# A hybrid decoder layer: attention takes the later chunk of each pair first, and chunk 2 is the last through the output stage

## The chip, the cores and the metric

The kernel runs on one core of one Trainium2 chip. The time is that of one execution on the device in microseconds; the median of three runs of the kernel before is 2466.35 us (2465.81 to 2468.02). The profile is of one further execution, which took 2469.59 us.

## The reference

One layer on a sequence of 2048 tokens of width 1024, all in float32. Cut to what matters:

```python
proj = x @ W_in                 # q, k, v (8 heads x 64), conv gates B, C, h, pooling input p
# attention, causal: token t sees s < t
z = q k^T / 8
log_om = log_sigmoid(-z)        # where s < t, else 0
tail = reverse_cumsum(log_om) - log_om
a = exp(log_sigmoid(z) + tail)  # stick breaking: sigmoid(z) times the product of what follows
attn_out = a v
conv_out = B * conv3(C * h);  pool_out = (window means - p) @ pool_w * pool_scale
mix = rmsnorm_per_64(concat(attn_out, conv_out, pool_out)) * gain
x = layer_norm(2**0.25 * x + mix @ W_o)
x = layer_norm(2**0.25 * x + square(relu(x @ W_up)) @ W_down)
```

## The kernel before

**Tiling.** The 2048 tokens are four chunks of 512. Each float32 operand of a dense product is split into a high part (a ScalarE copy to the type float32r) and a low part (a subtraction on VectorE or GpSimd), and a product is three matmuls: high by high, high by low, low by high.

**Attention.** A head of chunk `c` walks over the key segments `c, c-1, ..., 0` (`head`). Each segment has four units (`unit`), one for each 128 queries: two score matmuls into a bank `z` (L433, two buffers), two sigmoids (L436, L438), a scan along the keys that makes the running product (L443 on the diagonal segment, L446 elsewhere, which carries on from the segment before and reads one column of `z` as a dummy operand), and a multiply on GpSimd (L448). Each segment also has four blocks (`block`): transposes (L465), the split (L468, L469) and two matmuls with the values into `o` (L470, L471). So a head of chunk 0, 1, 2, 3 has 4, 8, 12, 16 units. `run` lays units and blocks out alternately, blocks five units behind. A head's end is `finish` (L484, L485); each pair of heads is then normalised (`rms`) and written to the scratch `mscr`, but for the last pair of all, which stays on the chip.

**Scratch in memory.** The projections write q, k and v to scratch tensors (`qscr`, `kscr`, `vscr`), and attention loads them by head and segment.

**Order of the program.** For the pair of chunks (0, 1), then for (2, 3): `qkv` projects keys, queries and values for heads 0 to 3 and then for heads 4 to 7, each for the lower chunk first; then attention runs for heads 0 to 3 of each chunk and for heads 4 to 7 of each chunk. After both pairs come the conv and pooling mixers (`bchp`, pairs (0, 1) and (2, 3)), the output stages of the four chunks (`out_stage`: mix times W_o, residual, layer norm, rows to `x1scr`; for chunks 0 and 1 also the transposed operands of the up projection to `tscr`), the up projection (`Up`; it reads the rows of chunks 2 and 3 back while it works on the first half) and the down projection.

**What sets the order of work.** Each engine has one queue, worked in order. A planner builds these queues ahead of time: it walks a modelled timeline and at each step issues the ready instruction of the highest priority. Attention stands above the dense products (`tc.high_priority(PRIO)`), and what evacuates a bank, loads operands or normalises stands above attention (`early`); within a class the order of the program decides. So projections, mixers and output stages fill TensorE wherever attention isn't ready. All DMAs are issued from SP's queue.

**The last output stage.** `out_stage(c)` for the last chunk loads seven of its eight mix tiles ahead (`ready`), does two banks of products on these seven, then takes the last pair's normalised product from the chip (`last_mix`, L512 to L514, in the buffers of the mix tiles), closes attention's pools and starts the up projection's loads. The first four output weights take the buffers of chunk 2's input tiles (`load_wo`); they are asked for where the last group of projections reaches the last chunk.

Of the kernel before, what the change touches and what calls it, by code (L numbers as in the profile page):

```python
# [22 lines left out]
NC = S // CH  # L23
HEADS = 8
HD = 64
ND = D // P
# [10 lines left out]
EORDER = (4, 5, 6, 7, 0, 1, 2, 3)  # L37
WINDOWS = (2, 4, 8, 16)
PRIO = 1 << 20
B11, T2, B21, T3, T1, T4, B22 = LOADS = range(7)  # L40
EARLY, LATE = 4, 6


def build(nc, tc, ctx, A, out):
# [78 lines left out]
    with ExitStack() as up:  # L123
        pools = phase1(nc, tc, ctx, up, A, ident, scr, hscr, split, rsqrt, layer_norm, bcast)
# [3 lines left out]
def phase1(nc, tc, whole, ctx, A, ident, scr, hscr, split, rsqrt, layer_norm, bcast):  # L128
# [39 lines left out]
    def early():  # L168
        return tc.high_priority(2 * PRIO)

# [32 lines left out]
    def defer(fn, groups):  # L203
        later.append([groups, fn])

    def tick():
        for item in later:
            item[0] -= 1
        while later and later[0][0] <= 0:
            later.pop(0)[1]()  # L210

    def dense_ps():
        return ppd.tile([P, CH], F, name="dn", tag="dn", bufs=2)
# [13 lines left out]
    def proj_t(xs, g):  # L227
        for c, w, x in operands(xs, g):
            for e in range(2):
                es = slice(e * P, (e + 1) * P)  # L230
                ps = dense_ps()
                for d in range(ND):
                    wh, wl = (t[:, d % 2, es] for t in w[d // 2])
                    xh, xl = x[d]
                    nc.tensor.matmul(ps, wh, xh, start=(d == 0), stop=False)  # L235
                    nc.tensor.matmul(ps, wh, xl, start=False, stop=False)  # L236
                    nc.tensor.matmul(ps, wl, xh, start=False, stop=(d == ND - 1))  # L237
                yield c, e, ps
                tick()
# [34 lines left out]
    def qkv(cs):  # L274
        xs = [(c, []) for c in cs]
        for g in range(2):
            proj_qk(xs, 2 + g, kscr, None)
            proj_qk(xs, g, qscr, 0.125)
            proj_v(xs, g)
# [31 lines left out]
    def bchp(chunks):  # L311
        x = [(c, []) for c in chunks]
        ys = {}
        mixers = {6: gate_b, 7: gate_c, 8: conv, 9: pool}
        for k, g in enumerate(GROUPS):
            for c, i, ps in proj_t(x, g):
                if c == NC - 1 and i == 0 and k == 3:
                    load_wo(EORDER[:4])
                with early():
                    mixers[g](c, i, ps, ys)  # L320
# [63 lines left out]
    def attention(c, pairs):  # L384
        for i in pairs:
            mix = {}
            for hh in range(2):
                head(c, 2 * i + hh, mix)

    def run(end=False):  # L390

        while units:
            units.pop(0)()
            turn[0] += 1
            if turn[0] > 5:
                blocks.pop(0)()
        while end and blocks:
            blocks.pop(0)()
            turn[0] = 0
        while end and soon:  # L400
            soon.pop(0)[1]()
# [89 lines left out]
    def load_wo(part):  # L491
        with early():
            w = [[load(A["w_o"][e][:, dd * CH:(dd + 1) * CH], "x", [P, CH], 2 * ND) for e in part] for dd in range(2)]
        wo.extend(zip(*w))

    def halves(name, tags, bufs=1):
        t = []
        for i, tag in enumerate(tags):
            h = pd.tile([P, CH], F, name=f"{name}_{i}", tag=tag, bufs=bufs)
            nc.sync.dma_start(h, A[name][i * CH:(i + 1) * CH].partition_broadcast(P))  # L500
            t.append(h)
        return t

    mix = {}

    def load_mix(c, part):
        with early():
            mix.setdefault(c, []).extend(load(mscr[c][e], "w", [P, CH], ND) for e in part)

    def last_mix(y):  # L510
        h = pm.tile([P, CH], R, name="mh", tag="wh", bufs=ND)
        nc.scalar.copy(h, y)  # L512
        l = pm.tile([P, CH], R, name="ml", tag="wl", bufs=ND)
        nc.vector.tensor_tensor(l, y, h.bitcast(F), ALU.subtract)  # L514
        mix[NC - 1].append((h, l))

    def out_product(c, ps, t, dd, part):
        ts = slice(t * P, (t + 1) * P)
        for i in part:
            (wh, wl), (mh, ml) = wo[i][dd], mix[c][i]  # L520
            nc.tensor.matmul(ps, mh[:, ts], wh, start=(i == 0), stop=False)
            nc.tensor.matmul(ps, mh[:, ts], wl, start=False, stop=False)
            nc.tensor.matmul(ps, ml[:, ts], wh, start=False, stop=(i == ND - 1))
# [1 line left out]
    g1, b1 = [], []  # L525

    def out_stage(c):
        ready = {0: 4, NC - 1: ND - 1}.get(c, 0)
        if c:
            load_mix(c, EORDER[:ready or ND])  # L530
        head = [dense_ps() for dd in range(2)] if ready else []
        for i, ps in enumerate(head):
            out_product(c, ps, i // 2, i % 2, range(ready))
        heads = len(head) // 2
        if c == NC - 1:
            pend.pop(0)(lambda fn: fn(), last_mix)
            att.close()
            ff.append(Up(nc, tc, whole, ctx, A, ident, x1scr, tscr, hscr))
            with early():
                ff[0].begin(pd)  # L540
        for t in range(4):
            r = pd.tile([P, D], F, name="r", tag="big", bufs=3)
            row = c * CH + t * P
            ld = nc.sync.dma_start(r, A["x"][row:row + P, :])
            if c == NC - 1:
                if t < 3:
                    with tc.issue_after(ld.ins):
                        ff[0].load(0, t)
            for dd in range(2):
                gs = slice(dd * 512, (dd + 1) * 512)  # L550
                ps = head.pop(0) if head else dense_ps()
                out_product(c, ps, t, dd, range(ready if t < heads else 0, ND))
                with early():
                    nc.vector.scalar_tensor_tensor(r[:, gs], r[:, gs], ALPHA, ps, ALU.mult, ALU.add)
                tick()
            if not g1:
                while later:
                    tick()
                g1.extend(halves("ln1_g", ("sqb0", "sqb1")))
                b1.extend(halves("ln1_b", ("rmsby", "rmsby"), 2))  # L560
            with early():
                layer_norm(pd, r, g1, b1)
                nc.sync.dma_start(x1scr[c][t], r)
            if c < 2:
                defer(lambda r=r, t=t: turn_out.rows(c, t, [r[:, 0:CH], r[:, CH:D]]), 2)
# [7 lines left out]
    for cs in ((0, 1), (2, 3)):  # L573
        qkv(cs)
        with tc.high_priority(PRIO):
            for pairs in ((0, 1), (2, 3)):
                for c in cs:
                    attention(c, pairs)
            run(True)
    for chunks in ((0, 1), (2, 3)):  # L580
        bchp(chunks)
    load_mix(0, EORDER)
    load_wo(EORDER[4:])
    with tc.high_priority(PRIO):
        while len(pend) > 1:
            pend.pop(0)(lambda fn: fn())
    ff = []
    for c in range(NC):
        out_stage(c)
    ff = ff[0]  # L590
    xw.close()
# [370 lines left out]
```

## Time and profile before

| | us |
|---|---|
| median of three runs | 2466.35 |
| lowest, highest | 2465.81, 2468.02 |
| profiled execution | 2469.59 |
| its span | 2467.8 |
| TensorE busy | 2404.1 |
| VectorE busy | 1590.3 |
| GpSimd busy | 1138.4 |
| ScalarE busy | 990.2 |
| mean granted clock of TensorE, as a share | 0.992 |

The span runs from the first to the last instruction of the profiled execution. Busy time is the union of an engine's instructions; the matmuls are pipelined, so that one whose own duration is 0.39 us can start 0.23 us after the one before.

### The profile page before, as it was taken

How to read it: one execution, taken by the hardware profiler on the slowest of the kernel's cores; microseconds unless marked ns; L12 is line 12 of the kernel's file. 1: busy time of each engine (PE TensorE's matmuls, PEld its weight loads, DVE VectorE, ACT ScalarE, POOL GpSimd, SP SyncE). 2: the span in 40 equal slices, each digit the busy share in tenths (PEclk: the TensorE clock that was granted, in tenths of full speed). 3: DMA queues.
4: the chain of work that ended last, by engine and by line, in shares of the span. 5: the costliest groups of instructions: out<-in, count | busy, mean ns of one | idle time of the engine just before them, and what ended most of it. 6: DMA issues, size and time to landing. Idle time of an engine off the chain costs nothing.

```text
span 2467.8 us, 33076 instructions
## 1 busy us (share of the span) xinstructions
PE 2404.1 (97%) x11728; PEld 1998.2 (81%) x11728; DVE 1590.3 (64%) x2243; ACT 990.2 (40%) x1913; POOL 1138.4 (46%) x833
## 2 busy tenths in 40 slices
PE   8999999999999999999999999999999999999997
PEld 6988888778778787788887888888778888888886
DVE  3778777888888899975767556655334333333367
ACT  4667666655765756512333222222112111111123
POOL 2557554864874856534656545554111101101137
PEclk9999999999999999999999999999999999999999
DMA  8658555623523456567665383333543212212212
GB/s 243 194 150 242 155 146 143 194 79 93 155 80 99 149 156 216 186 247 271 218 210 191 113 330 133 111 104 115 166 163 102 77 60 86 86 46 78 82 60 111
DMA packets 164854, 360.36 MB, mean 146 GB/s; under 512 B 18641, under 2 KB 35025, under 8 KB 162897
## 3 DMA queue, kind: packets, MB, share of 16 engines
q1 hardware_dynamic: 164688, 358.25, 45.3%
q8 instruction: 93, 1.52, 0.3%
q14 instruction: 73, 0.59, 0.1%
HBM read 245.19 MB, written 112.98 MB: 145 GB/s over the span
## 4 chain that ended last, share of the span: by engine, by line
PE 79%; DVE 9%; DMA 4%; POOL 3%; issue 3%; ACT 2%; SPq 1%; DVEq 0%; ACTq 0%; POOLq 0%
PE dn L891 8%; PE dn L893 8%; PE dn L892 8%; PE b L789 7%; PE c L789 4%; PE a L789 4%; PE z L433 4%; PE dn L235 3%; PE tp L465 3%; PE dn L237 3%; PE dn L236 3%; PE b L792 3%; PE c L792 2%; PE a L792 2%; PE o L471 2%
## 5 line engine op out<-in xcount | busy, mean ns | idle before, releaser
L448 POOL TENSOR_TENSOR g<-g,sig 128x512 f32<-128x512 f32 (+2 forms) x320 | 379.9, 1192 | 340.6 <-DVE g L446 154.5
L891 PE MATMUL dn<-d,ht 128*128 128x512 f32 x1024 | 399.6, 390 | 5.7 <-DVE y L895 3.2
L892 PE MATMUL dn<-d,ht 128*128 128x512 f32 x1024 | 399.1, 390 | 0.0
L893 PE MATMUL dn<-d,ht 128*128 128x512 f32 x1024 | 397.9, 390 | 0.5 <-DVE ht L869 0.5
L729 POOL TENSOR_TENSOR w<-raw,w 128x512 fp32r<-128x512 f32 x186 | 259.4, 1401 | 232.6 <-ACT w L728 232.5
L897 DVE TENSOR_TENSOR y<-dn,y 128x512 f32<-128x512 f32 x224 | 153.9, 688 | 323.8 <-PE dn L893 323.6
L855 POOL TENSOR_TENSOR d<-draw,d 128x1024 fp32r<-128x1024 f32 x32 | 76.7, 2411 | 518.4 <-ACT d L854 509.4
L446 DVE TENSOR_TENSOR_SCAN g<-beta,g,z 128x513 f32<-128x513 f32 x192 | 243.9, 1275 | 48.3 <-ACT sig L438 46.3
L868 ACT CAST ht<-draw 128x512 fp32r<-128x512 f32 x128 | 74.2, 620 | 447.2 <-PE dn L893 370.0
L436 ACT ACTIVATE beta<-z 128x512 f32<-128x512 f32 (+2 forms) x320 | 172.7, 540 | 164.3 <-PE z L433 152.5
L891 PEld LDWEIGHTS dn<-d,ht 128*128 128x128 f32 x1024 | 192.6, 188 | 47.7 <-DVE y L895 4.7
L893 PEld LDWEIGHTS dn<-d,ht 128*128 128x128 f32 x1024 | 192.7, 188 | 41.0 <-DVE ht L869 0.9
L892 PEld LDWEIGHTS dn<-d,ht 128*128 128x128 f32 x1024 | 192.6, 188 | 39.8
L728 ACT CAST w<-raw 128x512 fp32r<-128x512 f32 x186 | 114.4, 621 | 262.8 <-PE b L792 146.7
L235 PE MATMUL dn<-xh,wh 128*128 128x512 f32 x512 | 206.5, 406 | 8.0 <-ACT xh L182 4.9
L433 PE MATMUL z<-k,q 128*128 128x512 f32 (+3 forms) x640 | 193.5, 382 | 17.3 <-DVE g L446 13.0
L236 PE MATMUL dn<-xl,wh 128*128 128x512 f32 x512 | 206.6, 404 | 0.2 <-POOL xl L184 0.2
L237 PE MATMUL dn<-xh,wl 128*128 128x512 f32 x512 | 206.6, 404 | 0.0
L469 DVE TENSOR_TENSOR tl<-tp,th 128x512 fp32r<-128x512 f32 (+1 forms) x320 | 184.2, 595 | 32.0 <-ACT th L468 31.0
L465 PE MATMUL tp<-ident,g 128*128 128x128 f32 x1088 | 191.8, 275 | 2.0 <-POOL g L448 1.0
L789 PE MATMUL b<-x,w 128*128 128x512 f32 x768 | 190.1, 390 | 3.7 <-DVE u L796 2.1
L468 ACT CAST th<-tp 128x512 fp32r<-128x512 f32 (+1 forms) x320 | 161.6, 536 | 66.3 <-PE tp L465 53.9
(194 smaller groups left out, 4967.0 us busy)
## 6 DMA issues: line engine op xcount, KB each, us to landing
hscr<-h SPq DMA_DIRECT2D x128, 256.0 KB, 2.7
draw<-hscr SPq DMA_DIRECT2D x64, 512.0 KB, 4.0
raw<-in_w_up SPq DMA_DIRECT2D x62, 512.0 KB, 4.2
x<-tscr SPq DMA_DIRECT2D x14, 2048.0 KB, 13.1
wraw<-in_w_in SPq DMA_DIRECT2D x80, 256.0 KB, 3.3
k<-kscr SPq DMA_DIRECT2D x80, 256.0 KB, 3.1
v<-vscr SPq DMA_DIRECT2D x80, 256.0 KB, 2.9
xraw<-in_xt SPq DMA_DIRECT2D x64, 256.0 KB, 3.1
```

Of the source, the lines that this page charges most:

```text
L235: nc.tensor.matmul(ps, wh, xh, start=(d == 0), stop=False)
L236: nc.tensor.matmul(ps, wh, xl, start=False, stop=False)
L237: nc.tensor.matmul(ps, wl, xh, start=False, stop=(d == ND - 1))
L433: nc.tensor.matmul(z[:, 0:w], q[:, b, j * P:(j + 1) * P], m["k"][:, 0:w], start=(b == 0), stop=(b == 1))
L446: nc.vector.tensor_tensor_scan(left, rev, idle, st["prev"][j][:, OFF - 1:OFF], ALU.mult, ALU.bypass)
L448: nc.gpsimd.tensor_tensor(gv, gv, sig[:, 0:w], ALU.mult)
L465: nc.tensor.transpose(out=tp[:, j * P:(j + 1) * P], in_=m["g"][j][:, cols], identity=ident)
L729: self.nc.gpsimd.tensor_tensor(w[:, 1], src, w.bitcast(F)[:, 0], ALU.subtract)
L789: nc.tensor.matmul(ps, wk[:, 0, d], x[:, i, :, d, :], start=(first and d == 0 and i == 0), stop=False, skip_group_check=True)
L891: nc.tensor.matmul(ps, hh[:, ts], dh[:, ds], start=(i == 0), stop=False)
L892: nc.tensor.matmul(ps, hh[:, ts], dl[:, ds], start=False, stop=False)
L893: nc.tensor.matmul(ps, hl[:, ts], dh[:, ds], start=False, stop=(i == 3))
```

## The change

A constant `LAST = 2` replaces `NC - 1` (3) as the chunk whose output stage comes last: in the place where the output weights are asked for, in `last_mix` and in `out_stage`. The output stages run in the order 0, 1, 3, 2. Attention walks over a pair of chunks in reverse: 3 before 2, and, since the same loop serves both pairs, 1 before 0.

```diff
+LAST = 2
...
-                if c == NC - 1 and i == 0 and k == 3:
+                if c == LAST and i == 0 and k == 3:
                     load_wo(EORDER[:4])
...
-        mix[NC - 1].append((h, l))
+        mix[LAST].append((h, l))
...
-        ready = {0: 4, NC - 1: ND - 1}.get(c, 0)
+        ready = {0: 4, LAST: ND - 1}.get(c, 0)
...
-        if c == NC - 1:
+        if c == LAST:
             pend.pop(0)(lambda fn: fn(), last_mix)
...
-            if c == NC - 1:
+            if c == LAST:
                 if t < 3:
                     with tc.issue_after(ld.ins):
                         ff[0].load(0, t)
...
             for pairs in ((0, 1), (2, 3)):
-                for c in cs:
+                for c in cs[::-1]:
                     attention(c, pairs)
...
-    for c in range(NC):
+    for c in (0, 1, 3, 2):
         out_stage(c)
```

## Rows read from the trace of the kernel before

**Rows 1.** The page's first part: busy us, share of the span, instructions.
```profile
PE 2404.1 (97%) x11728; PEld 1998.2 (81%) x11728; DVE 1590.3 (64%) x2243; ACT 990.2 (40%) x1913; POOL 1138.4 (46%) x833
```

**Rows 2.** Busy time of each engine by stretch (us from the span's start).
```profile
core 0: us, PE busy (x) PEld busy (x) DVE busy (x) ACT busy (x) POOL busy (x), PEclk, DMA share, GB/s
78.00:198.00 120.00, 120.00 (x745) 106.44 (x745) 96.34 (x133) 81.10 (x179) 66.10 (x57) 1.00 0.62 171
331.00:455.00 124.00, 124.00 (x750) 108.47 (x749) 90.65 (x120) 83.52 (x173) 73.86 (x61) 1.00 0.60 164
455.00:850.00 395.00, 373.55 (x1911) 300.44 (x1909) 332.56 (x456) 245.29 (x497) 265.48 (x206) 0.98 0.36 112
850.00:1030.00 180.00, 172.87 (x897) 140.69 (x897) 173.65 (x254) 111.62 (x223) 114.42 (x90) 0.99 0.58 187
1030.00:1127.00 97.00, 94.41 (x429) 77.47 (x428) 69.59 (x129) 17.32 (x30) 32.51 (x26) 1.00 0.59 212
1127.00:1736.00 609.00, 605.31 (x2695) 501.11 (x2694) 374.71 (x442) 190.07 (x327) 334.70 (x238) 1.00 0.52 180
1736.00:2406.00 670.00, 663.89 (x2916) 547.63 (x2915) 264.80 (x411) 113.58 (x177) 95.44 (x40) 1.00 0.28 91
```

**Rows 3.** Waits of TensorE from 455 to 1030: us in total, times, longest.
```profile
PE z L433 <- DVE g L446: 13.0, 15, 3.8
PE o L471 <- DVE tl L469: 2.7, 4, 1.2
```

**Rows 4.** The last step of a head (L485), by stretch: length, busy (count).
```profile
331.30:472.00 140.70, 2.72 (x4) 1.00 0.62 177
472.00:693.00 221.00, 2.72 (x4) 0.98 0.34 103
693.00:836.50 143.50, 2.72 (x4) 0.98 0.33 101
836.50:1050.00 213.50, 2.73 (x4) 0.99 0.57 185
```

**Rows 5.** SP's queue at the starts: issue time, its length, line, operation.
```profile
77.65 0.81 SPq L427 DMA_DIRECT2D v<-vscr  x2
...
92.59 0.93 SPq L258 DMA_DIRECT2D vscr<-vst  x2
...
95.55 0.32 SPq L427 DMA_DIRECT2D v<-vscr  x1
...
194.86 2.21 SPq L258 DMA_DIRECT2D vscr<-vst  x2
...
218.29 0.93 SPq L258 DMA_DIRECT2D vscr<-vst  x2
...
312.83 0.93 SPq L258 DMA_DIRECT2D vscr<-vst  x2
...
337.05 0.93 SPq L258 DMA_DIRECT2D vscr<-vst  x2
```

**Rows 6.** The chain of waits near 200 us, then TensorE's timeline there.
```profile
199.77 4.79 DMA v<-vscr
...
201.83 1.05 PE L290 MATMUL msp<-blk,sqa 128*128 128x2 f32 x8
204.69 0.60 PE L470 MATMUL o<-th,v 128*128 128x512 f32 x1 [1.81 <-DMA v<-vscr]
205.09 0.63 PE L471 MATMUL o<-tl,v 128*128 128x512 f32 x1
...
208.29 0.30 PE L251 MATMUL dn<-wl,xh 128*128 128x256 f32 x1
```

**Rows 7.** The end of attention: first and last start of four steps.
```profile
L485 DVE TENSOR_TENSOR mixr<-o,mixr x32: 655/688/696, 86.4 to 1048.8; 64x512 f32<-64x512 f32 x32
L302 DVE SCALAR_TENSOR_TENSOR oa<-mixr,gain,msp x16: 695/734/748, 114.6 to 1063.0; 128x512 f32<-128x512 f32 x16
L512 ACT CAST mh<-oa x1: 613/613/613, 1086.1 to 1086.1; 128x512 fp32r<-128x512 f32 x1
L521 PE MATMUL dn<-xh,mh x8: 389/389/389, 1090.7 to 1126.2; 128*128 128x512 f32 x8
```

**Rows 8.** DMA issues: count, size, median us from issue to landing.
```profile
xraw<-in_w_o SPq DMA_DIRECT2D x16, 256.0 KB, 3.0
```

**Rows 9.** SP's queue: the last write of rows and the first reads.
```profile
1135.01 0.33 SPq L563 DMA_DIRECT2D x1scr<-r  x1
...
1148.91 1.66 SPq L718 DMA_DIRECT2D r<-x1scr  x3
```

## The prediction

> **What bounds the kernel now.** I began with the page's first part: TensorE is busy for 2404.1 of 2467.8 us, and no other engine comes near [rows 1]. Then the table by stretch [rows 2], whose edges I set where the chain of waits and the timeline of each stage change hands: projections alone to 78 us; attention with projections beside it to 455; attention with the conv and pooling mixers beside it to 850; attention with the output stages of chunks 0 and 1 to 1030; the other output stages to 1127; then the up and the down projection. From 1127 to 1736 TensorE idles 3.7 us in 609. The change touches the program only ahead of 1127 us, so whatever it brings must come out of the stretches before.
>
> There the reader is to see two kinds of stretch. From 331 to 455 TensorE is busy for 124.00 of 124 us while VectorE stands at 73%: attention is not what limits, since each time it waits a projection fills TensorE. From 455 to 850 TensorE idles 21.4 us (395 less 373.55) at a clock of 0.98, and from 850 to 1030 it idles 7.1 us (180 less 172.87) with VectorE at 96% (173.65 of 180). Those 28.5 us are the largest sum that a better order of attention could reach. The waits of TensorE between 455 and 1030 say what they are: 13.0 us in 15 waits of the score matmul for the scan that still holds its bank [rows 3].
>
> Next is the order of the heads. The last step of each head falls four times into each of these stretches [rows 4]: chunk 2, heads 0 to 3, takes 140.7 us; chunk 3, heads 0 to 3, 221.0; chunk 2, heads 4 to 7, 143.5; chunk 3, heads 4 to 7, 213.5. By the code a head of chunk 2 has 12 units and one of chunk 3 has 16, so a unit takes 2.93, 3.45, 2.99 and 3.34 us. A pace that goes with the chunk would show in the sum whichever comes first, so by itself the exchange only moves these four blocks about.
>
> **The change part by part.** No instruction is added or taken away: the same 320 units, 768 output matmuls and loads. What changes is which may start when, and with it the order in which the planner lays down each engine's queue up to 1127 us. The loop that is turned around serves both pairs of chunks, so chunk 1 also goes ahead of chunk 0.
>
> *Start of attention.* The first head now needs the values of chunk 1, whose second write goes out at 92.59 us; their first load goes at 95.55, where chunk 0's went at 77.65 [rows 5]. Attention starts up to 17.9 us later. In the meantime TensorE has the value projection and the next group's keys, which it ran anyway: 120.00 of 120 us busy from 78 to 198 [rows 2]. The attention work that stood between these projections moves behind them, so they end sooner; and scores and scans may run ahead of the values. I take 10 us of delay, between 0 and 17.9, and 0 us of TensorE time; without that cover it would be the 10.
>
> *Second group of heads, and chunks 2 and 3.* Here the values wanted first are written at 218.29 in place of 194.86, and at 337.05 in place of 312.83 [rows 5]: 23.4 and 24.2 us later by the old timing. But while attention is late, TensorE does just those projections. With its time fully used, an attention that is 10 us behind means projections that are 10 us ahead, and both meet again at the same sum of work. So I do not add these two to the first delay: 0 us, with up to 47.6 us of further delay as the other end (a rival below).
>
> *A stall at the second group.* At 199.77 attention loads values that have just been written, and the load lands 4.79 us later. TensorE, its queue in order, stands before the matmul that reads them: idle from 202.88 (201.83 plus 1.05) to 204.69, and the next 512-column matmul starts 0.40 us after it, in place of about 0.23, until 208.3 [rows 6]. That is 1.8 us of waiting, and by the doubled spacing of some 3.6 us after it another 1.8. With projections ahead of attention this wait should shrink; with chunk 1 first it can also return, since its values are the last written. I take half: −1.8 us, within −3.6 (gone) and +7.2 (once more at each of two starts).
>
> *The contended stretches.* Ten microseconds more of attention lie in the stretches where TensorE idles 28.5 us in 575: 10 × 28.5/575 = +0.5 us, at most +0.9 for the whole 17.9, at least 0.
>
> *The end of attention.* The last head ends at 1048.8, its normalised product is ready at 1063.0, and nothing takes it before 1086.1, when a buffer of the stage before comes free; the first matmul on it is at 1090.7 [rows 7]. So the end may come 23.1 us later at no price: 10 us are hidden, the cost is 0, and each microsecond beyond 23.1 is paid in full, because all but two banks of the last stage lie behind that product. That the last head is now a shorter one (12 units) buys nothing for the same reason. The stage that now stands third (chunk 3) has its mix complete 48 units before the end, as chunk 2 had 64 units before: at 2.99 us a unit that is 143 us ahead, ample.
>
> *Loads of the output weights.* They are asked for three projection units earlier, but their tiles are those of chunk 2's input, free only after its last unit, and they stand at the same place in the order of loads: 0 us; 16 loads of 3.0 us [rows 8] would be visible for one landing, +3.0, at the worst.
>
> *Rows of chunk 2.* They are now written last, up to 1135.01 by the old timing, and are the first that the up stage reads, from 1148.91 [rows 9], 13.9 us later. The first read is of the first row tile, written long before the last. 0 us; if a read met its own write, one landing, a few microseconds, on a transpose that stands beside full TensorE work.
>
> The sum: −1.8 + 0.5 = −1.3 us. The profiled execution took 2469.59 us, 1.8 around its span and 3.2 above the median of 2466.35. So 2468.3 as a profiled run, and 2465 as a median.
>
> One rule of the skill would put the ceiling elsewhere. The Trainium skill (Perfetto Trace Analysis, Identifying the Most-Contended Engine) says that the busy share of matmuls misleads, since they are pipelined, and that the busy share of weight loads is the better measure. Weight loads are busy 300.44 of 395 us (76%) from 455 to 850 against 501.11 of 609 (82%) in the full stage after [rows 2]; by that rule some 30 us of the first stretch are open in place of 21.4, an estimate that neglects the different mix of tile sizes. The sum stays the same by both; the faster rival's third would be about 12 us in place of 9.5, so 2453 in place of 2456.
>
> **The rivals.**
>
> *Slower: the delays add up.* If attention waits anew at each of its three starts, 17.9 + 23.4 + 24.2 = 65.5 us come together, 42.4 above the 23.1 of room: 2507. With two of the three, 42 us, 19 are paid: 2484. For it: in each group chunk 1 (or 3) is projected behind chunk 0 (or 2). Against it: a late attention hastens the projections, as above. It decides once the last head ends later than about 1072 us. I give it 0.13.
>
> *Slower: a new order with new stalls.* The planner sets the order from modelled times, and TensorE stands in real time before whatever is at the head of its queue. The 13.0 us that scores wait for scans [rows 3] are such a misfit. A re-laid queue could have as much again where long heads of chunk 3 now meet the mixers: +13, so 2478. For it: chunk 3's first four heads ran slowest (3.45 us a unit) in that very stretch. Against it: half of them now run before 455, beside projections. 0.17.
>
> *Faster: the new order fits better.* Chunk 3's first heads now start at about 340 us, so some 115 us of their long units lie in the stretch where TensorE is full and VectorE at 73%, and chunk 2's shorter ones fall among the mixers. If a third of the 28.5 us of idle time goes, 9.5 us are gained: 2456. Against it: the same number of units must still pass the later stretches. 0.30.
>
> That the change does nothing in effect, because the planner starts chunk 2's or 0's heads first as before, I put at under 0.02; the time would be the median of before.
>
> **How the numbers follow.** My forecast (moved about, hidden) has 0.40, the faster rival 0.30, the slower ones 0.30 together. What a measurement can tell from no change is about 0.2%, 4.9 us. The forecast's own spread is 2460 to 2470; a little of it on the fast side passes the bound, and some of each rival falls short of theirs: faster 0.33, same 0.37, slower 0.30. The range takes in 2456 and 2478 with the unknown terms beside them (−3.6 and +7.2 at the stall, +3.0 at the weights): 2450 to 2482, leaving out the added delays of 2484 and up.
>
> **What would show it.** Values of chunk 1 loaded first, near 85 to 95 us, with TensorE full from 78 to 198: the first step. No wait of TensorE for loaded values near 200 us, or a longer one: the stall. Last head ending between 1050 and 1072 us and the last product still waiting for its buffer: the room at the end. Idle time of TensorE from 455 to 1030 within 4 us of 28.5: the forecast against the second and third rivals. The up and down stages must keep their 609 and 670 us; if they do not, I missed a dependence there. I am wrong outright if attention ends past 1072 us with TensorE idle before the last stage, or if the stretch before 1127 is over 5 us shorter or longer.

## The result, and the profile after

The changed kernel takes 2482.86 us (median; 2479.59 to 2489.49) beside 2466.42 (2465.81 to 2468.02) for the kernel before: a ratio of 1.0073, 95% interval 1.0054 to 1.0092. It is 16.4 us slower where I had forecast no change. The profiled execution took 2484.28 us. In the fences of this kernel line numbers above L40 are one higher than in those of the kernel before (L433 is L434).

The page of the changed kernel, first part (busy time, share of the span, instructions), answers to [rows 1]:

```profile
span 2482.5 us, 33058 instructions
PE 2408.2 (97%) x11728; PEld 1999.2 (81%) x11728; DVE 1579.8 (64%) x2243; ACT 986.6 (40%) x1913; POOL 1144.1 (46%) x833
```

The span is 14.7 us longer, with the same number of instructions on each engine. The table by stretch, of the same kernel, answers to four rows of [rows 2] (columns as there; the up and down stages shifted by the 15.0 us by which they start later):

```profile
78.00:198.00 120.00, 119.73 (x743) 105.90 (x742) 86.89 (x117) 75.21 (x167) 60.31 (x53) 1.00 0.64 177
331.00:455.00 124.00, 123.78 (x738) 107.21 (x737) 92.55 (x118) 83.36 (x167) 72.94 (x58) 1.00 0.54 147
1142.00:1751.00 609.00, 606.66 (x2708) 502.32 (x2707) 378.42 (x443) 190.33 (x328) 337.51 (x239) 1.00 0.52 180
1751.00:2421.00 670.00, 662.77 (x2906) 546.67 (x2905) 262.70 (x411) 113.08 (x177) 93.20 (x40) 0.99 0.28 91
```

The up and down stages are as before (606.66 busy for 605.31, 662.77 for 663.89). All of the difference lies ahead of them. To find where, I cut both traces at the same events rather than at the same times: the first value projection, the first key projection of chunk 2, its counterpart for heads 4 to 7, the last value projection, the middle of the mixers, the last projection, the last head, the last output product. The first fence is the kernel before, the second the changed one; the first pair of numbers is the stretch and its length, the next TensorE's busy time.

```profile
0.00:55.90 55.90, 47.95 (x192) 37.40 (x193) 20.77 (x38) 24.26 (x39) 14.39 (x20) 1.00 0.82 235
55.90:212.90 157.00, 155.19 (x1014) 140.81 (x1013) 122.87 (x168) 103.33 (x234) 88.60 (x78) 0.99 0.67 189
212.90:332.70 119.80, 119.76 (x738) 105.66 (x737) 94.46 (x131) 81.97 (x177) 72.08 (x60) 1.00 0.63 179
332.70:454.50 121.80, 121.80 (x734) 106.39 (x733) 89.97 (x118) 81.53 (x170) 71.66 (x60) 1.00 0.60 163
454.50:648.40 193.90, 180.79 (x915) 145.28 (x915) 162.01 (x218) 116.17 (x235) 126.75 (x99) 0.97 0.36 112
648.40:846.90 198.50, 192.31 (x997) 155.13 (x996) 168.57 (x236) 126.57 (x258) 136.18 (x106) 0.98 0.36 112
846.90:1048.80 201.90, 191.41 (x986) 155.24 (x985) 191.57 (x282) 121.89 (x243) 124.84 (x98) 0.99 0.57 186
1048.80:1126.70 77.90, 76.52 (x344) 63.15 (x343) 54.15 (x104) 10.09 (x17) 25.13 (x20) 1.00 0.61 221
```

```profile
0.00:59.80 59.80, 49.23 (x192) 38.19 (x193) 21.00 (x38) 23.69 (x39) 14.40 (x20) 0.97 0.77 216
59.80:209.70 149.90, 147.74 (x954) 132.41 (x954) 107.01 (x147) 92.90 (x206) 76.94 (x67) 1.00 0.65 180
209.70:339.10 129.40, 126.30 (x781) 110.13 (x780) 101.20 (x148) 87.94 (x199) 82.52 (x69) 1.00 0.64 180
339.10:467.20 128.10, 125.75 (x742) 108.83 (x741) 96.10 (x120) 84.13 (x169) 74.38 (x59) 0.99 0.57 156
467.20:656.90 189.70, 181.44 (x930) 146.31 (x930) 160.17 (x222) 118.23 (x243) 129.54 (x102) 0.98 0.39 117
656.90:862.60 205.70, 191.38 (x985) 155.20 (x984) 167.13 (x235) 125.25 (x255) 138.86 (x107) 0.98 0.35 107
862.60:1068.70 206.10, 196.67 (x1010) 160.18 (x1009) 190.11 (x295) 121.32 (x245) 126.62 (x100) 0.98 0.58 189
1068.70:1142.00 73.30, 71.79 (x322) 59.20 (x321) 49.70 (x93) 8.95 (x15) 21.99 (x18) 1.00 0.61 221
```

Length less busy time is TensorE's idle time. Before, stretch by stretch: 7.95, 1.81, 0.04, 0.00, 13.11, 6.19, 10.49, 1.38, in all 41.0 us. After: 10.57, 2.16, 3.10, 2.35, 8.26, 14.32, 9.43, 1.51, in all 51.7. So 10.7 of the 15.3 us by which the output products end later (1142.0 less 1126.7) are idle time. No one stretch holds them: the first gives 2.6, the two in which TensorE had no idle time give 5.4, the first half of the mixers takes back 4.9 and the second half gives 8.1. The other 4.6 us are matmuls at a wider spacing, and 3.4 of them are the granted clock: read in windows of 1 us, busy time times what the clock lacks of 1.00 makes 15.0 us up to the last output product, where it made 11.6 before. Of these 3.4 us, 1.7 lie in the first stretch (0.97 for 1.00). The last 1.2 us are not placed.

What TensorE waits for, in us in total, times and longest. First the kernel before from 56 to 455 us, where this is its only wait, then the changed kernel from 59 to 467:

```profile
PE o L470 <- DMA v<-vscr: 1.8, 1, 1.8
```

```profile
PE z L434 <- DVE g L447: 3.0, 3, 2.1
PE o L472 <- DVE tl L470: 1.8, 3, 1.1
PE z L434 <- ACT sig L439: 1.1, 1, 1.1
PE o L471 <- ACT th L469: 0.9, 2, 0.5
PE o L471 <- DMA v<-vscr: 0.5, 1, 0.5
```

The reader is to see that the one stall I had priced (values just written) nearly went, and that nine small waits on attention's own chain came: a score for a bank that a scan or a sigmoid holds, an output product for its operand's high or low part. Each stands where the next instruction of TensorE's queue isn't ready; whether other work was ready just then, the rows do not say. Over the whole run the waits of scores for scans grew from 13.0 to 16.0 us, and those of output products for low parts from 3.8 to 9.2.

The end of attention, by first and last start, answers to [rows 7]:

```profile
L486 DVE TENSOR_TENSOR mixr<-o,mixr x32: 655/688/696, 116.5 to 1068.7; 64x512 f32<-64x512 f32 x32
L513 ACT CAST mh<-oa x1: 616/616/616, 1101.4 to 1101.4; 128x512 fp32r<-128x512 f32 x1
L522 PE MATMUL dn<-xh,mh x8: 389/389/389, 1105.9 to 1141.6; 128*128 128x512 f32 x8
```

The last head ends 19.9 us later and its product is taken 32.7 us after that: still not what the last stage waits for.

### The profile page after: what moved, and what is told of

The parts are those of the page before. It is cut to its first block, busy times and chain, and to the rows that moved or that the text cites. A ratio compares the mean times of both kernels' runs of the same rounds, so it can differ in the third digit from the quotient of the medians.

```text
span 2482.5 us, 33058 instructions
## 1 busy us (share of the span) xinstructions
PE 2408.2 (97%) x11728; PEld 1999.2 (81%) x11728; DVE 1579.8 (64%) x2243; ACT 986.6 (40%) x1913; POOL 1144.1 (46%) x833
## 4 chain that ended last, share of the span: by engine, by line
PE 76%; DVE 10%; DMA 5%; POOL 3%; issue 3%; ACT 2%; SPq 0%; DVEq 0%; ACTq 0%; POOLq 0%
PE dn L892 8%; PE dn L894 8%; PE dn L893 8%; PE b L790 6%; PE c L790 4%; PE a L790 4%; PE z L434 3%; PE dn L236 3%; PE dn L237 3%; PE dn L238 3%; PE b L793 3%; PE tp L466 3%; PE c L793 2%; PE a L793 2%; PE o L472 2%
## 5 line engine op out<-in xcount | busy, mean ns | idle before, releaser
L449 POOL TENSOR_TENSOR g<-g,sig 128x512 f32<-128x512 f32 (+2 forms) x320 | 386.2, 1211 | 343.5 <-DVE g L447 143.7
L434 PE MATMUL z<-k,q 128*128 128x512 f32 (+3 forms) x640 | 193.4, 383 | 20.9 <-DVE g L447 16.0
L470 DVE TENSOR_TENSOR tl<-tp,th 128x512 fp32r<-128x512 f32 (+1 forms) x320 | 185.2, 595 | 25.7 <-ACT th L469 24.9
```

The source lines that it names most:

```text
L434: nc.tensor.matmul(z[:, 0:w], q[:, b, j * P:(j + 1) * P], m["k"][:, 0:w], start=(b == 0), stop=(b == 1))
L449: nc.gpsimd.tensor_tensor(gv, gv, sig[:, 0:w], ALU.mult)
```

## The experiments

Two theories stood against each other. **Lateness**: attention starts later, since the chunk it takes first is projected last, and the delay is paid somewhere. **New queue**: no delay is paid; the planner lays the engines' queues down anew, and the new ones meet the chip's real times worse than the old ones. In the expectations, A and D are forms of Lateness and B is New queue; C puts the whole cost on the turn of chunks 2 and 3, and E on the long heads of chunk 1 ahead of the short ones of chunk 0. Each TensorE queue written out has some 8,100 rows; "lines of difference" below are rows removed and rows added against the kernel before, counted together (a row that moves counts twice, so 16,200 would be all). "Idle" is TensorE's idle time up to the last output product, found as above.

**Which part of the change costs.** The exchange has two parts, chunk 3 ahead of 2 and chunk 1 ahead of 0. `only23` keeps the first alone, in the changed kernel:

```
-                for c in cs[::-1]:
+                for c in (cs if cs[0] == 0 else cs[::-1]):
```

> Chunk 3 ahead of chunk 2 and the output stages in the order 0, 1, 3, 2 as in the change, but chunk 0 ahead of chunk 1 as before. The change cost about 14.7 us between the two profiled executions; counted against each matmul's own steady spacing, TensorE lost 3.8 us more before 62 us, 4.6 more from 186 to 248 and 7 more from 807 to 931. Theory A (the two starts of chunk 1 are to blame for the first two): the first two go, the third stays: about +6 to +8 us over the kernel before, 2473. Theory B (the new order of the queues, whatever it is, meets other stalls): no such split; anything from -5 to +20. Theory C (the turn in the pair 2, 3 is all of it): +14 to +17, 2482.

Measured: 2469.24 us (2467.68 to 2469.74), ratio 1.0011 (1.0002 to 1.0020); idle 42.1. `only01` puts the second part alone into the kernel before:

```
-                for c in cs:
+                for c in (cs[::-1] if cs[0] == 0 else cs):
```

> Chunk 1 ahead of chunk 0, but chunk 2 ahead of chunk 3 and the output stages in order as before. Theory A: both early losses are there (one 3.4 us wait for a bank near 36 us, short waits from 195 to 245), and little else: +8 us, 2474. Theory B: anything from -5 to +20, and the two halves don't add up to the whole. Theory C: +-3, 2466.

Measured: 2480.45 (2477.88 to 2481.57), ratio 1.0053 (1.0036 to 1.0070); idle 49.8. So in the queues laid down here, what the change is named after costs 2.8 us, and the turn of chunks 0 and 1, which came with the shared loop, 14.0. Theories A and C miss both times. Theory B allows both, but its halves were not to add up to the whole, and here they do: 16.8 us for 16.4.

`proj_rev` is the changed kernel with the projections turned too, so that the chunk wanted first is also the one whose values are written first:

```
-        qkv(cs)
+        qkv(cs[::-1])
```

> The changed kernel, with the projections of each pair also taken in reverse (chunk 1 ahead of 0, 3 ahead of 2), so that the values that attention wants first are again those written first. Theory A (attention asks for what is projected last): the first values are loaded near 78 us again, the early losses of 8.4 us go, about 2474. Theory B: the losses move elsewhere, no sure sign. Theory C: stays at 2480 or above.

Measured: 2478.71 (2474.66 to 2480.36), ratio 1.0046 (1.0031 to 1.0061); idle 49.3. Most of the loss (12.3 of 16.4 us) stays when the values come early, at 81.35 us for 99.26 in the changed kernel; Theory A had looked for 2474. `swap_pairs`, the kernel before with head pairs 0 and 1, and 2 and 3, exchanged, was to be a new order of equal work:

```
-            for pairs in ((0, 1), (2, 3)):
+            for pairs in ((1, 0), (3, 2)):
-EORDER = (4, 5, 6, 7, 0, 1, 2, 3)
+EORDER = (4, 5, 6, 7, 1, 0, 3, 2)
```

> The kernel before with no chunk exchanged: only the two pairs of heads of a group trade places (heads 2, 3 ahead of 0, 1, and 6, 7 ahead of 4, 5), with the mix tiles summed in that order. Every head has the same work, the same chunk order and the same dependences on projections. Theories A and C: no reason for a difference, within 3 us of 2466. Theory B: a new plan alone moves the time by 5 to 15 us, either way.

Measured: 2465.66 (2460.14 to 2473.40), ratio 0.9994 (0.9981 to 1.0007); idle 40.5. It tests less than I meant: the queues of the four computing engines come out the same instruction for instruction, only with other heads' addresses. What it shows is that the same queue gives the same time.

**Is it lateness?** `proj01_rev` turns only the projections of chunks 0 and 1, in the kernel before, so that attention gets the wrong chunk first there:

```
-        qkv(cs)
+        qkv(cs[::-1] if cs[0] == 0 else cs)
```

> The kernel before with attention in its own order (chunk 0, then 1), but the projections of the pair 0, 1 reversed, so that chunk 0's values are written last and attention starts late for that reason alone. Theory D (an attention that starts late leaves VectorE idle early, and the lack is paid later, where VectorE is 96% busy beside the output stages): the start is some 15 us late, the last head ends near 1060, about +8 to +14 us, 2477. Theory E (it is the long heads of chunk 1 ahead of the short ones of chunk 0 that disturb the queues, not the lateness): within 3 us of 2466.

Measured: 2475.02 (2474.20 to 2480.43), ratio 1.0035 (1.0024 to 1.0046); idle 50.7. By the time alone this is Theory D's forecast (+8 to +14 us), and Theory E misses. `early_v` goes the other way: query and value projections alternate chunk by chunk, so values come early. The two functions become generators that yield after each chunk (those lines are left out here).

```
...
-            proj_qk(xs, g, qscr, 0.125)
-            proj_v(xs, g)
+            for step in zip(proj_qk(xs, g, qscr, 0.125), proj_v(xs, g)):
+                pass
...
```

> The kernel before with the query and value projections of a group taken by chunk: q of the lower chunk, v of the lower chunk, q of the upper, v of the upper (before: both q, then both v). Chunk 0's values are ready two query projections (10.9 us of matmuls) sooner, and so are chunk 2's. Theory D turned round: an attention that starts earlier ends earlier, and time is gained: last head near 1038, -4 to -9 us, 2460. Theory E: within 3 us of 2466.

Measured: 2484.85 (2482.95 to 2486.42), ratio 1.0070 (1.0049 to 1.0090); idle 51.7. The last step of a head and the matmuls on the last product, first and last start, first in `proj01_rev`, then in `early_v`:

```profile
L485 DVE TENSOR_TENSOR mixr<-o,mixr x32: 654/688/695, 108.8 to 1077.6; 64x512 f32<-64x512 f32 x32
L521 PE MATMUL dn<-xh,mh x8: 389/389/389, 1098.7 to 1133.9; 128*128 128x512 f32 x8
```

```profile
L489 DVE TENSOR_TENSOR mixr<-o,mixr x32: 653/688/696, 81.1 to 1045.0; 64x512 f32<-64x512 f32 x32
L525 PE MATMUL dn<-xh,mh x8: 389/389/389, 1106.9 to 1141.9; 128*128 128x512 f32 x8
```

`early_v` starts and ends its heads earlier than the kernel before (81.1 for 86.4, 1045.0 for 1048.8) and loses 18.4 us, where Theory D had a gain of 4 to 9 and Theory E no change; `proj01_rev` ends them 28.8 us later and loses 8.6. So a loss as large as the change's needs no lateness. That some of the 8.6 us in `proj01_rev` is lateness is not excluded.

`g0_rev` and `g1_rev` turn chunks 0 and 1 for heads 0 to 3 alone and for heads 4 to 7 alone:

```
+                for c in (cs[::-1] if cs[0] + pairs[0] == 0 else cs):            # g0_rev
+                for c in (cs[::-1] if cs[0] == 0 and pairs[0] == 2 else cs):     # g1_rev
```

> The kernel before with chunk 1 ahead of chunk 0 for heads 0 to 3 alone (the first start, at 60 to 95 us). Theory D: most of the cost of reversing the pair 0, 1 (13.9 us) is here, since this is where nothing else is left for attention to do: +8 to +13, 2477. If the second start (the values near 200 us) carries it: +2 to +4, 2470.

> The kernel before with chunk 1 ahead of chunk 0 for heads 4 to 7 alone (the second start, near 200 us). Theory D: attention has caught up with the projections there (a load of just written values stalls it already), so it is late by some of the 23 us between the two chunks' values: +2 to +6, 2470. If the second start carries it all: +10 to +14, 2478.

Measured: `g0_rev` 2483.59 (2478.34 to 2484.18), ratio 1.0060 (1.0038 to 1.0082), idle 53.4; `g1_rev` 2474.15 (2470.31 to 2477.65), ratio 1.0024 (1.0012 to 1.0036), idle 47.3. The halves lose 17.2 and 7.7 us by their medians, together 24.9, where both at once lose 14.0. Costs that belong to each half by itself would add up; these don't. (A delay that both halves share would not add up either, so this alone does not decide.) Neither half falls where Theory D put it, +8 to +13 and +2 to +6.

**The old order of chunks, laid down anew.** If the queues are the cause, edits that leave the order of chunks alone must cost as much. `START` is a counter value at which the low parts of operands change the rule by which they are dealt to VectorE or GpSimd: 46 in place of 40 changes the engine of at most six of them (VectorE's instructions are 2,245 for 2,243), 37 and 43 of at most three. `lag6` lets attention's blocks run one unit further behind.

```
-START = 40
+START = 46        # start46; start37, start43 and start34 likewise
-            if turn[0] > 5:
+            if turn[0] > 6:        # lag6
```

> The kernel before with no chunk exchanged: of the loads numbered 40 to 45 alone, the low part is made by the other of VectorE and GpSimd (a constant of 40 becomes 46). No dependence changes, no work is moved by more than six operations of about 1 us, and attention starts as before; but the planner's queue for TensorE then differs from the old one over more than half its length (6185 lines of difference of some 8100, from line 898 on, before the second start). Theory B (the queues of the kernel before fit the chip better than a queue planned anew, and every new plan pays 5 to 15 us in TensorE's waits): +5 to +15, 2476, with the waits of the second matmul on values (for ScalarE's and VectorE's split) grown. Theory A or D (order and lateness of attention): within 3 us of 2466.

> As the run before, with the constant at 37: loads 37 to 39 alone change engine. TensorE's queue differs in 6838 lines. Theory B: +5 to +15, 2476. Theories A and D: within 3 us of 2466.

> The kernel before with attention's blocks six units behind the scores in place of five: one unit more in flight, the same work and chunk order. TensorE's queue differs in 6610 lines. Theory B: +5 to +15 like any new plan. Theories A and D: attention starts at the same time and waits less for its split, so 0 to -5 us, 2464.

Measured: `start46` 2476.00 (2475.24 to 2476.73), ratio 1.0044 (1.0029 to 1.0059), 6,185 lines, idle 45.5. `start37` 2481.88 (2479.11 to 2484.61), 1.0064 (1.0045 to 1.0083), 6,838 lines, idle 51.6. `lag6` 2489.18 (2488.31 to 2490.85), 1.0098 (1.0083 to 1.0113), 6,610 lines, idle 56.4. (The 6,185 lines are 38% of the queue, removed and added rows being counted together; "more than half" in the expectation counted them once.) The three edits, none of which has to do with the exchange, cost 9.6, 15.5 and 22.8 us against 2466.42. Theories A and D had looked for none. Theory B has the direction, but 15.5 and 22.8 lie above its 5 to 15, and the waits that it named did not grow in `start46` (output products for low parts 4.1 us for 3.8, scores for scans 6.0 for 13.0). Attention's end in `lag6`:

```profile
L485 DVE TENSOR_TENSOR mixr<-o,mixr x32: 654/688/696, 87.3 to 1040.1; 64x512 f32<-64x512 f32 x32
L521 PE MATMUL dn<-xh,mh x8: 389/389/389, 1112.9 to 1147.7; 128*128 128x512 f32 x8
```

The slowest kernel of all has the earliest end of attention.

> The kernel before with the constant at 43: TensorE's queue differs from the old one in 786 lines alone and comes back to it. Theory B: a queue that stays nearly the same costs nearly the same, within 4 us of 2466. If changing the engine of a load is what costs in itself (the constants 37 and 46 did 15 and 10 us): +5 or more, 2473.

> The kernel before with the constant at 34: 7518 lines of difference. Theory B: +5 to +20, 2479. If the cost came with particular loads near number 40 to 45: no reason for more than 3 us.

Measured: `start43` 2470.54 (2466.12 to 2473.75), ratio 1.0014 (1.0005 to 1.0023), only 786 lines, idle 45.0; `start34` 2484.60 (2481.06 to 2485.62), 1.0072 (1.0057 to 1.0087), 7,518 lines, idle 49.4. A queue that stays nearly the same keeps nearly the same time (4.1 us above 2466.42, just over the 4 of Theory B), and the three changed engines of `start43` cost a quarter of what the three of `start37` do: it isn't the change of engine that costs.

**The new order of chunks, laid down anew.** The same constant in the changed kernel, and in `only23`:

> The changed kernel with the constant at 46: again a new plan (6866 lines of difference to the changed kernel's) for the same order of chunks. Theory B: the cost of the change is that of a plan, so it moves: anywhere from 2470 to 2490, with no reason to stay at 2482. Theories A and D: the cost is in the order of chunks and stays, 2480 to 2485.

> The changed kernel with the constant at 34, a third plan of the new order. Theory B (the order has no cost of its own): it falls among the re-planned kernels of the old order, 2474 to 2489. If the new order has a cost of its own of 10 us or more on top of the plan's: 2485 to 2500.

> The turn of chunks 3 and 2 alone (it cost 2.7 us), with the constant at 46 (which cost 9.6 us alone and changes the queues from about 165 us on). Theory B: the early queue goes, and the cost with it rises to that of a new plan: 2474 to 2486. If the turn of 3 and 2 is free whatever the plan, and costs add: 2479.

Measured: `after_start46` 2483.61 (2478.15 to 2484.54), ratio 1.0070 (1.0052 to 1.0088), idle 47.7 in an execution of 2478.15; `after_start34` 2472.18 (2470.75 to 2477.84), 1.0031 (1.0021 to 1.0041), idle 46.6; `only23_start46` 2473.59 (2469.57 to 2476.42), 1.0032 (1.0019 to 1.0045), idle 42.9. With the same exchange of chunks, `after_start34` is 10.7 us faster than the changed kernel, and the intervals of their ratios lie apart. The constant that costs the old order 18.2 us takes 10.7 from the new one. `after_start46` decides nothing: it lies where both theories allowed it. The other two lie a little below Theory B's ranges (2472.18 for 2474 to 2489, 2473.59 for 2474 to 2486), and far from the costs that would stay (2480 to 2485) or add (2479). Paired by the constant, the new order is 16.4 us (40) and 7.6 us (46) behind the old one and 12.4 us (34) ahead of it, 3.9 us behind on average, far inside that spread: a cost of the order itself is not shown, and one of a few us is not excluded. The row of `after_start34` for all that lies ahead of the last output product, then that of the changed kernel:

```profile
0.00:1133.30 1133.30, 1086.71 (x5905) 908.20 (x5906) 901.88 (x1289) 661.15 (x1365) 668.86 (x538) 0.99 0.53 161
```

```profile
0.00:1142.00 1142.00, 1090.30 (x5905) 910.45 (x5906) 892.41 (x1291) 662.41 (x1365) 665.24 (x536) 0.99 0.53 160
```

**All together.** Over the 18 kernels (both given ones and these 16) the medians go with TensorE's idle time, correlation 0.90; with the end of the last head it is −0.05. That the time goes with how the queues happen to fit is shown by the edits that change little but the queues; the correlation by itself says less, since idle time is a part of the time. Most of the rest of the spread is the clock: read in windows of 1 us as above, it takes 6.1 to 19.3 us in the 18 profiled executions, and the end of the last output product less idle time and less this lies between 1072 and 1081 us in all of them, where the ends themselves run from 1126 to 1148. How much of the clock's part belongs to the queue is open; the kernel before, too, had 0.996 in an execution of 2461.65 us and 0.991 in one of 2469.38. Which entries decide, and why the kernel before has so little idle time between 213 and 455 us, stays open. None of these queues beat the kernel before: `swap_pairs`, with its queue, ties, and the others lie 2.8 to 22.8 us behind, 12.4 on average.

## Why the prediction was wrong, point by point

*Start of attention: right in its cost, low in its size.* The first values are loaded at 99.26 us, by SP's queue of the changed kernel (issue time, length; it answers to [rows 5]):

```profile
93.06 0.93 SPq L259 DMA_DIRECT2D vscr<-vst  x2
99.26 0.81 SPq L428 DMA_DIRECT2D v<-vscr  x2
```

That is 21.6 us after the old 77.65, more than the 17.9 I held for the most; I had looked for it near 85 to 95. Yet from 78 to 198 TensorE is busy for 119.73 of 120 us: the projections cover it, as I wrote.

*Second group, chunks 2 and 3: right.* The further 47.6 us of delay did not come. Attention's end moved by 19.9 us, no more than the start.

*The stall near 200 us: right about the stall, wrong about its neighbourhood.* The load's wait shrank from 1.8 to 0.5 us, and the doubled spacing behind it went (granted clock 1.00 from 199 to 213), but two other waits came near 200 us:

```profile
200.20 0.33 PE L472 MATMUL o<-tl,v 128*128 128x128 f32 x1 [0.54 <-DVE tl L470]
204.32 0.73 PE L434 MATMUL z<-k,q 128*128 128x512 f32 x2 [1.12 <-ACT sig L439]
```

*The contended stretches: inside my margin.* From 455 to 1030 TensorE idles 31.3 us, within 4 of 28.5. But it hid a large exchange, −4.9 in the first half of the mixers and +8.1 in the second, and the margin tested the wrong place: 8.4 of the 10.7 us of new idle time lie ahead of the last value projection.

*The end of attention: right.* 1068.7 is within 1050 to 1072, and the last product waits for its buffer until 1101.4. The delay was twice the 10 us that I had taken, and the room just covered it: 22.4 us rather than 23.1, since 1063.0 is the start of a step of 0.73 us. *Output weights, up and down stages: right*; no wait of TensorE from 1000 to 1142 us is for a load, and from the last output product to the end the changed kernel takes 1340.5 us for 1341.1. (By the code the weights are asked for two projection units earlier, not three.) *Rows of chunk 2: right.* SP's queue of the changed kernel answers to [rows 9], with 12.5 us between the last write and the first read for 13.9:

```profile
1151.19 0.33 SPq L564 DMA_DIRECT2D x1scr<-r  x1
...
1163.73 1.54 SPq L719 DMA_DIRECT2D r<-x1scr  x3
```

**The step that failed** is the one on which the forecast rested: "by itself the exchange only moves these four blocks about". From it followed that a new order costs no more than its delay, and that projections would go on covering attention ahead of the mixers as they had in two stretches of [rows 2]. Those two stretches did stay full (0.27 us idle from 78 to 198, 0.22 from 331 to 455). The new idle time came where the sum had no term: 2.6 us ahead of the first value projection, 3.1 in five waits between 209.7 and 250 us, a part that [rows 2] leaves out, and 2.1 in one wait of a score for a scan at 458.94. The first row shows the second of these places in the changed kernel, the second row the third:

```profile
209.70:250.00 40.30, 37.20 (x195) 29.53 (x194) 30.15 (x41) 26.75 (x61) 28.44 (x23) 1.00 0.71 205
458.94 0.72 PE L434 MATMUL z<-k,q 128*128 128x512 f32 x2 [2.12 <-DVE g L447]
```

The contended stretches and what follows hold only 2.3 us more, net. The kernel before idles 0.04 us from 212.9 to 454.5. I took that cover for a property of the stages; it belonged to one set of queues. So the stretch before the up stage became 15.3 us longer, over the 5 that I had named as being wrong outright: 10.7 us of idle time and 3.4 of lower clock, where the sum had −1.3.

The rival "a new order with new stalls" is what happened. I gave it 0.17 and priced it at +13 us, by the 13.0 us of waits for scans [rows 3]; it was 16.4. That the price is near is luck: of the new waits those for scans make only 3.0 us, and those of output products for low parts 5.4. I also set its place wrongly: in these queues the long heads of chunk 3 among the mixers cost 2.8 us (`only23`), and the turn of chunks 0 and 1, which I priced at its delay alone, 14.0 (`only01`). One new wait stands even ahead of the first score matmul; the bracket is idle time and what ended it (changed kernel):

```profile
32.55 0.39 PE L238 MATMUL dn<-xh,wl 128*128 128x512 f32 x1
36.32 0.52 PE L236 MATMUL dn<-xh,wh 128*128 128x512 f32 x1 [3.38 <-DVE qk L67]
36.65 0.61 PE L237 MATMUL dn<-xl,wh 128*128 128x512 f32 x1
37.06 0.63 PE L238 MATMUL dn<-xh,wl 128*128 128x512 f32 x1
```

The wait is for a bank. ScalarE, which makes the high part from it before VectorE makes the low one, has a weight's cast ahead of that in its queue, and the cast waits for its load. ScalarE's rows in the changed kernel:

```profile
34.32 0.62 ACT L183 CAST wh<-wraw 128x512 fp32r<-128x512 f32 x1 [2.73 <-DMA wraw<-in_w_in]
34.84 0.58 ACT L66 CAST qk<-dn 128x512 fp32r<-128x512 f32 x1
```

In the kernel before ScalarE makes that part of `qk` at 32.30, and TensorE's wait for the bank is 1.05 us. TensorE's own order of instructions is the same in both kernels up to that point; it is ScalarE's queue that was laid down otherwise. That the planner took the load to be quicker than it is would explain the order; no run tested it.

My chances, too, leaned on the belief that a re-laid queue is as good as the old one on average (0.30 faster for a better fit). Of 16 re-laid queues none was faster.

## What to carry to other kernels

Where a planner lays down in-order queues, read "this engine is full here" as a statement about these queues, not about the stage: an edit that re-lays them, however small, can draw a new fit, and if the old one is good the draw is mostly a loss (here 12 us of 2466 on average). Before an exchange is blamed or praised, re-lay the old and the new order a few times by a constant that changes no work, and compare the groups; and look at everything that shares the loop being turned, since the part not in the change's name can hold most of the cost.

## What the runs showed that I had not expected

Kernels of the same arithmetic, with at most six small instructions on another engine, spread from 2466 to 2485 us by the order of the queues, and with attention's lag to 2489: 0.9%.

The 3.38 us wait above costs more than itself. The matmuls after it start 0.43 us apart up to 40 us, where they started 0.23 apart until 32.55, and the granted clock says the same (changed kernel; the clock is the number before the last two):

```profile
28.00:32.50 4.50, 4.50 (x19) 3.20 (x18) 2.25 (x3) 2.48 (x4) 1.29 (x1) 1.00 0.75 244
36.30:39.30 3.00, 2.98 (x8) 2.37 (x9) 2.01 (x3) 1.16 (x3) 1.02 (x1) 0.56 0.87 186
40.00:44.00 4.00, 4.00 (x19) 3.23 (x18) 0.00 (x0) 0.00 (x0) 0.00 (x0) 0.99 0.89 230
```

That is the lower of the two levels, 1.2 of 2.4 GHz, for most of 3 us. A shorter wait can be followed by the same. After the wait of 2.12 us that ends at 458.94 the changed kernel has the first row here; after the 1.81 us that end at 204.69 [rows 6] the kernel before has the second:

```profile
459.00:463.00 4.00, 4.00 (x19) 3.82 (x20) 4.00 (x6) 4.00 (x9) 1.66 (x2) 0.61 0.62 174
```

```profile
204.60:208.30 3.70, 3.60 (x13) 3.24 (x14) 1.44 (x4) 0.85 (x2) 3.70 (x4) 0.54 1.06 364
```

Yet another wait of 1.81 us in the kernel before, which ends at 20.97, left the clock at 1.00 up to 25 us. The length of a wait alone does not tell whether the clock falls after it.

The Trainium skill (TensorE: Matmul & The Clock Gate, A second HAM failure mode: psum-queue depth-cycling) says of one kernel that frequent, very short waits between groups of matmuls, at its banks, cost it throughput through the clock. The five waits of 0.37 to 1.07 us between 209.7 and 250 us of the changed kernel do not show it: the granted clock is 1.00 there.
